# A two-layer hybrid decoder trunk on one core: plain copies of queries and keys, 128-row score products, decay on ScalarE, and other estimates for the order of the mixer

## The chip, the cores and the metric

The kernel runs on one core of one Trainium2 chip. The metric is the device time of one execution in microseconds (us), less is better. The time before is the median of three runs; one more execution was taken with the hardware profiler, and all rows below are of that one.

## The reference

`x` is 512 tokens of 1024 float32 channels. Each of two layers runs a half-step SwiGLU feed-forward block (2816 wide), a token mixer, and a second feed-forward block, each followed by a layer norm of a scaled residual. The mixer has one input projection, three groups of heads, and one output projection:

```
aq, ak, av, bq, bk, bv, cc = jnp.split(x @ w_in[l], IN_SPLIT_IDX, axis=-1)
o_a = diff_attention(rope(aq), rope(ak), av, lam)        # 6 heads, two maps of 32 channels each
o_b = dilated_attention(rope(bq), rope(bk), bv)          # 6 heads of 64 channels
o_c, v_first = rwkv7_mixer(cc, ...)                      # 4 heads of 64 channels
mix = jnp.concatenate([o_a, o_b, o_c], axis=-1) @ w_out[l]
```

`diff_attention` is causal: softmax of the first map minus `lam` times that of the second, times the values. `dilated_attention` comes down to one causal softmax with a bias by distance. `rwkv7_mixer` is a recurrence over tokens, with `S_t = S_{t-1} (diag(w_t) - kk_t^T (a_t kk_t)) + v_t^T k_t`.

## The kernel before

Products keep float32 accuracy by splits: an operand is a high part (rounded to the type `FR`, fp32r) plus a low part, and a product is high x high + high x low + low x high, three products of TensorE (`mm3`). In the mixer the weights come through SP's queue (`wr`), ScalarE rounds the high part (`wh`) and POOL subtracts the low part (`wl`).

The feed-forward blocks are written in their order. The mixer isn't: it is 24 generators (list `RANK`), each of which yields what its next step needs (a tile, a free buffer, an event) and then issues that step. `Board.merge` runs them once, while the program is built. It keeps a clock for each engine and, by the estimates in `Watched.run` and `Board.note`, a time at which each tile is ready and each buffer is free. It takes the first generator in `RANK` whose needs are met by TensorE's planned time, or else the one whose needs are met first. So the estimates alone set the order of the instructions on all five queues, and each engine then works through its queue in that order. As all calls go through `Watched.run`, the profile puts nearly all of the mixer on one line, L511.

The steps that the change and the prediction touch:

- `columns`, `by_token`: the input projection, in products `p<-...` of 256 columns (groups A and B) and the main filling work of the mixer. `out` is the output projection, in products of 512 columns.
- `turner`: for each of 24 tiles `rc` of queries and keys, two transposes on TensorE, the split into `z` (high part on ScalarE, low on VectorE), and a store by SP into DRAM (`qkA`, `qkB`).
- `fetch`: POOL's queue brings the queries `q` and keys `k` of one head back, with high and low parts stacked on partitions, so that one product of 96 rows (A) or a pair of products (B) gives a split score. The tiles are of type `FR` and the DRAM tensor is float32. Four buffers `x` hold two heads. Group A has four copies for each head, group B three, of which the last brings the low keys into 64 rows.
- `attend`: for each head and each 128 queries, a unit of work: scores into `p`, VectorE adds the bias and finds the maximum (`t`, `nm`), ScalarE takes the exponential, TensorE transposes the result (`m<-kept,t`), ScalarE copies it to `aT`, TensorE multiplies by the values (`r<-v,aT`), VectorE scales (`o`) and ScalarE squares (`junk`). A layer has 24 units of group A and 24 of B.
- `scan`: the recurrence in 8 chunks of 64 tokens. Each chunk has three dependent steps: products into `z`, copied to `zs`; products with the inverse (`r<-zs,t16t`), copied with a changed sign into `uv`; products with `bt` into the new state `st`. `sgm` is the state times the decay of the next chunk, and the next state adds it. `rwkv_out` makes the chunk's output.

The second product of a unit of group B, and the decay:

```
pe.matmul(sc[:, :nn], a[:, 0, qs], a[:, 1, :nn], start=True, stop=False)
pe.matmul(sc[:, :nn], a[0:64, 0, qs], b[:, :nn], start=False, stop=True)
...
vec.tensor_scalar(sgm[:, j, :], nst[:, j, :], gam[j][:, ch + 1:ch + 2], None, op0=OP.mult)
```

Of the kernel before, what the change touches and what calls it, by code (L numbers as in the profile page):

```python
# [16 lines left out]
S = 512  # L17
# [352 lines left out]
class Board:  # L370
# [36 lines left out]
    def note(self, name, fn, aps, cost):  # L407
        at = self.free[name]
        tiles = [self.ready.setdefault(a.tensor.name, [0.0, "", 0.0, None]) for a in aps]
        assert all(r[3] != "dropped" for r in tiles)  # L410
        dma = fn == "dma_start"
        for r in tiles[dma and tiles[0][1] == "dma":]:
            if r[1] != name or name != "pe":
                at = max(at, r[0] + 0.134)
        end = at + cost
        self.free[name] = end
        if dma:
            n = 4
            for d in aps[0].shape:
                n *= d  # L420
            end = max(end, self.free["dma"]) + n / 340e3
            self.free["dma"] = end
            end += 2.0
        for r in tiles:
            r[2] = max(r[2], end)
        tiles[0][0] = max(tiles[0][0], end)
        tiles[0][1] = "dma" if dma else name
        if dma:
            self.late = max(self.late, end)
        elif name != "pe":  # L430
            self.last = max(self.last, end)
# [45 lines left out]
class Watched:  # L477
# [5 lines left out]
    def __getattr__(self, fn):  # L483
        call = getattr(self.engine, fn)

        def run(*args, **kw):
            aps = [a for a in list(args) + list(kw.values()) if hasattr(a, "tensor") and hasattr(a, "shape")]
            n = 1
            for a in aps:
                m = 1  # L490
                for d in a.shape[1:]:
                    m *= d
                n = max(n, m)
            if self.name == "pe":
                n = 1
                for d in aps[0].shape[1:]:
                    n *= d
                rate = 2 if fn == "transpose" else 1 if aps[2].dtype == FR and n >= 256 else 4
                cost = rate * n / 2400.0 + (0.009 if rate == 4 else 0.003)
            elif fn == "dma_start":  # L500
                cost = {"pool": 1.04, "act": 0.5, "sp": 0.47}[self.name]
            elif fn == "reciprocal":
                cost = 0.06 + n / 160.0
            else:
                cost = {"vec": 0.07 + n / 960.0, "act": 0.12 + n / 1400.0, "pool": 0.1 + n / 720.0}[self.name]
                if fn == "activation" and "accum_out" in kw:
                    cost += 0.1
                if fn == "tensor_tensor" and self.name == "pool":
                    cost = 0.1 + n / 450.0
            self.board.note(self.name, fn, aps, cost)  # L510
            return call(*args, **kw)  # L511

        return run
# [7 lines left out]
class Mix:  # L521
# [247 lines left out]
    def fetch(self):  # L769

        dma = self.gps.dma_start
        ap = lambda t, off, dims: bass.AP(tensor=t.tensor, offset=t.offset + off, ap=dims)
        for grp in "AB":
            for hp in range(3):
                for e in range(2):
                    yield f"qk{grp}{hp}", "x", "x"
                    if (hp, e) == (0, 0):
                        yield f"qk{grp}{hp}", "x", "x", "bias"
                        self.bias = self.get("bias", "bias")
                        dma(self.bias, self.tr.consts[:, 130:642] if grp == "A" else self.tr.consts[:, 642:1154])  # L780
                    a = self.get("x", "q", (128, 2, S), FR)
                    d = self.qk[grp, hp]
                    hi, lo, k = e * 64 * S, (256 + e * 64) * S, 128 * S
                    if grp == "A":
                        b = self.get("x", "k", (128, 2, S), FR)
                        dma(a[0:64], ap(d, hi, [[256 * S, 2], [2 * S, 32], [1, 2 * S]]))
                        dma(b[0:64], ap(d, hi + k, [[0, 2], [2 * S, 32], [1, 2 * S]]))
                        dma(a[64:96], ap(d, hi, [[2 * S, 32], [1, 2 * S]]))
                        dma(b[64:96], ap(d, lo + k, [[2 * S, 32], [1, 2 * S]]))
                    else:  # L790
                        b = self.get("x", "k2", (64, S), FR)
                        dma(a[:, 0, :], ap(d, hi, [[256 * S, 2], [S, 64], [1, S]]))
                        dma(a[:, 1, :], ap(d, hi + k, [[0, 2], [S, 64], [1, S]]))
                        dma(b, ap(d, lo + k, [[S, 64], [1, S]]))
                    self.qkt[grp, hp, e] = a, b
                    self.mark(f"q{grp}{hp}{e}")


# [307 lines left out]
    def scan(self):  # L1106

        vec, act, pe, sp = self.vec, self.act, self.pe, self.sp
        u, drop, kr, am, bt, yt, gam = self.u, self.drop, self.kr, self.am, self.bt, self.yt, self.gam
        st = None  # L1110
        yield "yt0"
        for ch in range(8):
            hf, cc = divmod(ch, 4)
            if cc == 0:
                yield "u", "u"
                for j in range(2):
                    kr[j, hf] = u("kr", (128, 4, 2, 64))
                    sp.dma_start(kr[j, hf].rearrange("p c e t -> p (c e t)"), self.kd[j, hf])
                yield f"yt{hf}", kr[0, hf], kr[1, hf]
            yield f"uv{ch // 2}"  # L1120
            uv, vt = self.uv[ch // 2]
            uvc = uv[:, ch % 2]
            heads = [(h, h // 2, HALF[h % 2], HALF[1 - h % 2], am[hf, h % 2, cc // 2][:, cc % 2, h // 2]) for h in range(4)]
            yield ".", "r"
            z = self.acc("r", (128, 2, 64))
            for h, j, s, f, a_ in heads:
                pe.matmul(z[f, j, :], a_[s, 0:64], uvc[s, h, :], start=True, stop=st is None)
                if st is not None:
                    pe.matmul(z[f, j, :], kr[j, hf][s, cc, 0, :], st[s, j, :], start=False, stop=True)
            zs = self.t("zs", (128, 2, 64), bufs=2)  # L1130
            act.copy(zs, z)
            drop(z)
            yield ".", "r"
            ups = self.acc("r", (128, 2, 64))
            for h, j, s, f, a_ in heads:
                pe.matmul(ups[f, j, :], yt[hf][f, cc * 2 + j, :], zs[f, j, :], start=True, stop=True)
            act.mul(uvc[HALF[1], 0::2], ups[HALF[1]], -1.0)
            vec.tensor_scalar(uvc[HALF[0], 1::2], ups[HALF[0]], -1.0, None, op0=OP.mult)
            drop(ups)
            nst = None  # L1140
            if ch < 7:
                yield ".", "r", "st"
                ps = self.acc("r", (128, 2, 64))
                for h, j, s, f, a_ in heads:
                    pe.matmul(ps[s, j, :], bt[hf, cc // 2][:, cc % 2, j, s], uvc[:, h, :], start=True, stop=True)
                nst = self.get("st", "st", (128, 2, 64))
                for j in range(2):
                    gj = gam[j][:, ch:ch + 1]
                    if st is None:
                        vec.tensor_scalar(nst[:, j, :], ps[:, j, :], gj, None, op0=OP.mult)  # L1150
                    else:
                        vec.scalar_tensor_tensor(nst[:, j, :], ps[:, j, :], gj, sgm[:, j, :], op0=OP.mult, op1=OP.add)
                drop(ps)
                if ch < 6:
                    sgm = self.t("sgm", (128, 2, 64), bufs=2)
                    for j in range(2):
                        vec.tensor_scalar(sgm[:, j, :], nst[:, j, :], gam[j][:, ch + 1:ch + 2], None, op0=OP.mult)
            if cc == 3:
                drop(yt[hf], bt[hf, 0], bt[hf, 1])
            self.chunks.append((ch, uv, st, heads, kr, vt, am))  # L1160
            self.mark(f"chunk{ch}")
            st = nst
# [62 lines left out]
    def attend(self, grp):  # L1225
# [6 lines left out]
        def scores(x):  # L1232
# [7 lines left out]
            for m in range(M):  # L1240
                sc = self.acc("p1")
                if isA:
                    pe.matmul(sc[:, :nn], a[0:96, m, qs], b[0:96, m, :nn], start=True, stop=True)
                else:
                    pe.matmul(sc[:, :nn], a[:, 0, qs], a[:, 1, :nn], start=True, stop=False)
                    pe.matmul(sc[:, :nn], a[0:64, 0, qs], b[:, :nn], start=False, stop=True)
                t = self.get("t", "t")
                nm = self.t("nm", (128, 1), bufs=8)
                vec.tensor_tensor_reduce(t[:, :n], sc[:, :n], bias[:, S - n:], scale, 3e38, op0=OP.add, op1=OP.min,
# [300 lines left out]
```

## Time and profile before

| | |
|---|---|
| median of three runs | 2336.14 us (2324.28 to 2336.32) |
| the profiled execution | 2317.18 us, span 2315.4 us |
| TensorE (PE) busy | 2210.5 us, 95% of the span, mean granted clock 0.974 |
| VectorE (DVE), ScalarE (ACT), GpSimd (POOL) busy | 1146.9, 803.2, 317.8 us |
| DMA | 258.34 MB, mean 112 GB/s |
| first mixer, second mixer | about 376 to 818 us, 1520 to 1968 us |

The span runs from the first to the last instruction of the profiled execution. A busy TensorE is not TensorE at its peak: a matmul at the lower clock, or one that is started late after the one before it, counts as busy. The list of waits puts idle time of an engine down to what ended it; in the list by lines and in the timeline a name such as `p<-k,q` reads output<-inputs, then the tile of the array (rows x columns), the shape, and the count. A float32 product that isn't `FR` is two rows in the trace, a transpose or an `FR` product one. Without that in mind, a mean over rows is half the time of such a product.

### The profile page before, as it was taken

The numbers are of one execution on the slowest core, as the hardware profiler recorded it, in microseconds if no ns is written. First come the engines' busy times: TensorE is split into PE (matmuls) and PEld (weight loads), VectorE is DVE, ScalarE is ACT, GpSimd is POOL, SyncE is SP. The second block draws the span as 40 slices with busy tenths as digits, with TensorE's granted clock in tenths as the row PEclk, the third lists the DMA queues.
The fourth block names the chain that finished last, engine by engine and source line by source line (L and its number), as shares of the span: only waits on it lengthen the run. The fifth ranks groups of instructions, "written<-read, shape, count | busy, mean of one in ns | idle before, by whom it ended". The sixth has DMA issues, their size and how long they took to land.

```text
span 2315.4 us, 31736 instructions
## 1 busy us (share of the span) xinstructions
PE 2210.5 (95%) x12384; PEld 1861.4 (80%) x12384; DVE 1146.9 (50%) x2483; ACT 803.2 (35%) x1559; POOL 317.8 (14%) x344
## 2 busy tenths in 40 slices
PE   9999999987899999999999999999878999999998
PEld 8888888787776788888888888887877867888886
DVE  3333337766666733333643332556665666333336
ACT  3332223434445322322433222343444443222222
POOL 1000002443222200000010000033432322000000
PEclk9999999998889999999999999999987999999999
DMA  5333344354533333332543333432554433333334
GB/s 171 100 97 103 105 137 155 101 136 84 117 93 107 110 91 91 100 100 91 173 120 103 102 101 109 152 131 86 134 107 96 107 95 119 86 97 91 100 109 155
DMA packets 265702, 258.34 MB, mean 112 GB/s; under 512 B 56314, under 2 KB 213056, under 8 KB 265552
## 3 DMA queue, kind: packets, MB, share of 16 engines
q1 hardware_dynamic: 221488, 228.20, 32.6%
q0 software_dynamic: 43488, 27.06, 5.7%
q8 instruction: 97, 1.59, 0.3%
q10 hardware_dynamic: 576, 1.05, 0.1%
q14 instruction: 53, 0.43, 0.1%
HBM read 233.85 MB, written 22.28 MB: 111 GB/s over the span
## 4 chain that ended last, share of the span: by engine, by line
PE 82%; DVE 8%; DMA 5%; issue 3%; POOL 1%; ACT 1%; SPq 0%; DVEq 0%; POOLq 0%; ACTq 0%
PE p L86 18%; PE p L87 18%; PE p L85 18%; PE p L511 14%; PE r L511 4%; PE m L511 4%; DMA k<-qkA 3%; PE r L86 2%; PE r L87 2%; PE r L85 2%; DMA k<-qkB 1%; DVE x L511 1%; POOL wl L511 1%; DVE xlo L511 1%; DVE gy L511 0%
## 5 line engine op out<-in xcount | busy, mean ns | idle before, releaser
L80 DVE TENSOR_TENSOR lo<-raw,hi 128x1024 fp32r<-128x1024 f32 x300 | 366.1, 1223 | 626.8 <-ACT hi L79 626.6
L86 PE MATMUL p<-xlo,hi 128*128 128x512 f32 (+1 forms) x1392 | 534.7, 384 | 0.7 <-DVE xlo L126 0.7
L85 PE MATMUL p<-xhi,hi 128*128 128x512 f32 (+1 forms) x1392 | 531.4, 382 | 0.5 <-ACT xhi L125 0.5
L87 PE MATMUL p<-xhi,lo 128*128 128x512 f32 (+1 forms) x1392 | 531.6, 382 | 0.0
L79 ACT CAST hi<-raw 128x1024 fp32r<-128x1024 f32 x300 | 315.1, 1052 | 582.7 <-PE p L86 256.6
L85 PEld LDWEIGHTS p<-xhi,hi 128*128 128x128 f32 x1392 | 261.3, 188 | 55.9 <-ACT xhi L125 1.0
L86 PEld LDWEIGHTS p<-xlo,hi 128*128 128x128 f32 x1392 | 261.5, 188 | 52.4 <-DVE xlo L126 1.1
L87 PEld LDWEIGHTS p<-xhi,lo 128*128 128x128 f32 x1392 | 261.5, 188 | 51.2
L511 POOL TENSOR_TENSOR wl<-wr,wh 128x512 fp32r<-128x512 f32 x152 | 204.1, 1363 | 670.8 <-ACT wh L511 639.5
L511 PE MATMUL p<-wh,xhi 128*128 128x256 f32 (+1 forms) x704 | 234.0, 332 | 2.3 <-DVE rb L511 2.0
L511 PE MATMUL p<-wh,xlo 128*128 128x256 f32 (+1 forms) x704 | 219.1, 311 | 0.5 <-DVE xlo L511 0.4
L511 PE MATMUL p<-wl,xhi 128*128 128x256 f32 (+1 forms) x704 | 218.7, 311 | 0.0
L86 PE MATMUL p<-lo,hh 128*128 128x512 f32 x528 | 205.8, 390 | 0.0
L87 PE MATMUL p<-hi,hl 128*128 128x512 f32 x528 | 205.8, 390 | 0.0
L85 PE MATMUL p<-hi,hh 128*128 128x512 f32 x528 | 205.7, 390 | 0.0
L511 PEld LDWEIGHTS p<-wh,xhi 128*128 128x128 f32 x704 | 139.7, 198 | 13.7 <-PE p L511 2.3
L511 PEld LDWEIGHTS p<-wh,xlo 128*128 128x128 f32 x704 | 139.1, 198 | 7.6 <-DVE xlo L511 2.2
L246 DVE TENSOR_TENSOR hr<-p,hr 128x512 f32<-128x512 f32 x88 | 60.8, 691 | 166.9 <-PE p L87 156.7
L511 PEld LDWEIGHTS p<-wl,xhi 128*128 128x128 f32 x704 | 139.5, 198 | 4.3
L247 ACT CAST hh<-hr 128x512 fp32r<-128x512 f32 x88 | 54.3, 618 | 205.8 <-DVE hr L246 195.8
L511 ACT ACTIVATE t<-t,nm 128x128 f32<-128x128 f32 (+3 forms) x144 | 80.1, 557 | 120.7 <-DVE nm L511 119.7
L85 PEld LDWEIGHTS p<-hi,hh 128*128 128x128 f32 x528 | 99.1, 188 | 20.5
(253 smaller groups left out, 3054.6 us busy)
## 6 DMA issues: line engine op xcount, KB each, us to landing
raw<-in_ffn_a_down SPq DMA_DIRECT2D x66, 512.0 KB, 3.3
raw<-in_ffn_b_down SPq DMA_DIRECT2D x66, 512.0 KB, 3.3
raw<-in_ffn_a_gate SPq DMA_DIRECT2D x44, 512.0 KB, 3.8
raw<-in_ffn_a_up SPq DMA_DIRECT2D x44, 512.0 KB, 3.8
raw<-in_ffn_b_gate SPq DMA_DIRECT2D x40, 512.0 KB, 3.8
raw<-in_ffn_b_up SPq DMA_DIRECT2D x40, 512.0 KB, 3.8
wr<-in_w_in SPq DMA_DIRECT2D x56, 256.0 KB, 3.2
wr<-in_w_in SPq DMA_DIRECT2D x24, 512.0 KB, 3.7
```

The lines of the kernel that those rows point to most:

```text
L79: nc.scalar.copy(hi, raw)
L80: (vec or nc.vector).tensor_tensor(lo, raw, hi.bitcast(FT), op=OP.subtract)
L85: mm(out, lh, rh, start=first, stop=False)
L86: mm(out, lh, rl, start=False, stop=False)
L87: mm(out, ll, rh, start=False, stop=last)
L246: nc.vector.tensor_tensor(hr, acc[1, f], hr, op=OP.mult)
L247: nc.scalar.copy(hi, hr)
L511: return call(*args, **kw)
```

## The change

Queries and keys are copied into float32 tiles, which are then read as `FR` without a conversion. In group B the low keys are copied twice, into 128 rows, and the second product of a unit takes 128 rows: the high and low parts of the query times the low part of the key. The decay `sgm` is a scaled copy on ScalarE. And the planner's estimates for TensorE, for transfers, and for POOL's issues are others.

```
-            end = max(end, self.free["dma"]) + n / 340e3
+            end = max(end, self.free["dma"]) + n / 300e3
...
-                rate = 2 if fn == "transpose" else 1 if aps[2].dtype == FR and n >= 256 else 4
-                cost = rate * n / 2400.0 + (0.009 if rate == 4 else 0.003)
+                if fn != "transpose" and aps[2].dtype == FR and n >= 256:
+                    cost = n / 2286.0 + 0.0055
+                else:
+                    m = 1
+                    for d in aps[1].shape[1:]:
+                        m *= d
+                    cost = max(n, m) / 1200.0 + 0.004
...
-                cost = {"pool": 1.04, "act": 0.5, "sp": 0.47}[self.name]
+                cost = {"pool": 0.65, "act": 0.5, "sp": 0.47}[self.name]
...
-                    a = self.get("x", "q", (128, 2, S), FR)
+                    a = self.get("x", "q", (128, 2, S))
...
-                        b = self.get("x", "k", (128, 2, S), FR)
+                        b = self.get("x", "k", (128, 2, S))
...
-                        b = self.get("x", "k2", (64, S), FR)
+                        b = self.get("x", "k2", (128, S))
...
-                        dma(b, ap(d, lo + k, [[S, 64], [1, S]]))
-                    self.qkt[grp, hp, e] = a, b
+                        dma(b, ap(d, lo + k, [[0, 2], [S, 64], [1, S]]))
+                    self.qkt[grp, hp, e] = a.bitcast(FR), b.bitcast(FR)
...
-                        vec.tensor_scalar(sgm[:, j, :], nst[:, j, :], gam[j][:, ch + 1:ch + 2], None, op0=OP.mult)
+                        act.activation(sgm[:, j, :], nst[:, j, :], AF.Copy, scale=gam[j][:, ch + 1:ch + 2])
...
-                    pe.matmul(sc[:, :nn], a[0:64, 0, qs], b[:, :nn], start=False, stop=True)
+                    pe.matmul(sc[:, :nn], a[:, 0, qs], b[:, :nn], start=False, stop=True)
```

How this moves instructions shows at two places. The first is TensorE's queue at the end of the second layer's scan. Before, the last step of its second chunk from the end (`r<-uv,bt`) stood amid the scores of group B (`q`, `k_16199`), between the products with the inverse and the transposes of a unit:

```order
L511 MATMUL r<-zs,t16t 64x64 x4
L511 MATMUL m<-kept,rc 128x128 x2
L511 MATMUL m<-kept,o 128x128 x4
L511 MATMUL p_16367<-q 128x256
L511 MATMUL p_16367<-k_16199,q 128x256
L511 MATMUL r<-uv,bt 64x64 x4
L511 MATMUL m<-kept,t 128x128 x2
```

Now it stands behind the last score, and three products of the output projection are what lies between the steps:

```order
L516 MATMUL m<-kept,o 128x128 x4
L516 MATMUL r<-zs,t16t 64x64 x4
L516 MATMUL p_16224<-wh,xhi 128x512
L516 MATMUL p_16224<-wl,xhi 128x512
L516 MATMUL p_16224<-wh,xlo 128x512
L516 MATMUL r<-uv,bt 64x64 x4
```

So the two last chunks of that scan have moved behind the attention of group B.

The second place is ScalarE's queue in the first layer's scan, where `sgm` now stands between the square of one unit and the split of the next turned tile, with exponentials (`t,l<-t,nm`) around it:

```order
L516 ACTIVATE t,l<-t,nm 128x256 x2
L516 COPY aT<-m 128x512
L516 ACTIVATE junk,ssA<-r 128x64
L516 ACTIVATE sgm<-st,gam 128x64 x2
L516 CAST z<-m 128x256
L516 CAST wh<-wr 128x512 x2
L516 ACTIVATE t,l<-t,nm 128x384 x2
```

Before, a row `TENSOR_SCALAR sgm<-st,gam 128x64 x2` stood in VectorE's queue, right behind the new state.

## Rows read from the trace of the kernel before

**Rows 1.** The page: busy time, share of the span and instructions of each engine.

```profile
PE 2210.5 (95%) x12384; PEld 1861.4 (80%) x12384; DVE 1146.9 (50%) x2483; ACT 803.2 (35%) x1559; POOL 317.8 (14%) x344
```

**Rows 2.** Stages: length, busy PE, PEld, DVE, ACT, POOL; clock, DMA, GB/s.

```profile
376.00:818.00 442.00, 397.20 (x2994) 345.51 (x2993) 290.24 (x878) 186.41 (x527) 144.47 (x149) 0.94 0.41 110
818.00:1520.00 702.00, 701.42 (x3189) 581.14 (x3188) 281.75 (x362) 211.74 (x250) 13.61 (x22) 1.00 0.37 112
1520.00:1968.00 448.00, 402.98 (x3003) 348.30 (x3002) 291.67 (x884) 190.91 (x532) 143.59 (x146) 0.94 0.42 108
```

**Rows 3.** TensorE's waits: us in total, times, longest.

```profile
PE p L511 <- DMA k<-qkA: 39.7, 6, 11.0
...
PE r L511 <- ACT junk L511: 4.9, 4, 2.2
...
PE p L511 <- DMA k<-qkB: 0.5, 2, 0.3
```

**Rows 4.** TensorE's timeline at the two longest waits (start, duration; idle before).

```profile
548.59 0.77 PE L511 MATMUL p<-k,q 96*128 96x256 f32 x2 [11.03 <-DMA k<-qkA]
...
1699.86 0.77 PE L511 MATMUL p<-k,q 96*128 96x256 f32 x2 [10.87 <-DMA k<-qkA]
```

**Rows 5.** Eight short stretches of the mixers, with columns as in rows 2.

```profile
504.00:512.00 8.00, 4.83 (x28) 4.82 (x29) 3.48 (x18) 2.23 (x9) 0.00 (x0) 0.79 0.65 125
548.00:556.00 8.00, 7.41 (x45) 7.37 (x46) 4.77 (x20) 3.21 (x12) 0.00 (x0) 0.59 0.18 51
592.00:604.00 12.00, 12.00 (x77) 11.32 (x75) 8.27 (x32) 5.79 (x20) 2.69 (x2) 0.57 0.06 17
632.00:648.00 16.00, 15.68 (x97) 12.05 (x96) 6.02 (x29) 6.45 (x22) 1.72 (x2) 0.57 0.29 64
1656.00:1664.00 8.00, 6.38 (x29) 6.31 (x30) 4.10 (x22) 2.77 (x11) 0.00 (x0) 0.57 0.66 111
1700.00:1708.00 8.00, 8.00 (x66) 7.87 (x67) 4.68 (x20) 3.52 (x15) 0.00 (x0) 0.69 0.17 45
1740.00:1752.00 12.00, 9.63 (x67) 9.05 (x68) 5.92 (x27) 5.00 (x18) 0.25 (x1) 0.61 0.18 49
1780.00:1800.00 20.00, 19.53 (x113) 15.61 (x114) 7.75 (x33) 8.28 (x28) 2.71 (x2) 0.57 0.31 63
```

**Rows 6.** DMA issues on POOL's queue: count, size, median us to landing.

```profile
x<-x POOLq DMA_DIRECT2D x8, 512.0 KB, 4.1
...
k<-qkA POOLq DMA_DIRECT2D x12, 256.0 KB, 12.8
...
bias<-in_constants POOLq DMA_DIRECT2D x4, 256.0 KB, 3.4
```

**Rows 7.** Chain, 527 to 552 us; then POOL by line (count, busy us, mean ns).

```profile
529.39 18.95 DMA k<-qkA
...
L511 POOL DMA_DIRECT2D k<-qkA x24 | 15.4, 641 | 0.0
```

**Rows 8.** TensorE's timeline in group B, layer 0, 714 to 722 us.

```profile
714.63 1.00 PE L511 MATMUL r<-v,aT 128*128 128x64 f32 x8
...
717.66 0.36 PE L511 MATMUL p<-q 128*128 128x256 f32 x1
717.95 0.38 PE L511 MATMUL p<-k,q 64*128 64x256 f32 x1
718.26 0.55 PE L511 MATMUL m<-kept,t 128*128 128x128 f32 x3
```

**Rows 9.** The same for group A, layer 1, 1706 to 1725 us.

```profile
1714.47 0.40 PE L511 MATMUL p<-k,q 96*128 96x256 f32 x2
1714.71 0.49 PE L511 MATMUL m<-kept,t 128*128 128x128 f32 x3
```

**Rows 10.** VectorE's timeline, 622 to 634 us; then ScalarE by line, first mixer.

```profile
626.48 3.95 DVE L511 TENSOR_SCALAR sgm<-st,gam 128x64 f32<-128x64 f32 x2
...
L511 ACT ACTIVATE uv<-r 64x128 f32<-64x128 f32 x8 | 2.2, 272 | 2.3 <-PE r L511 2.1
```

## The prediction

> **What bounds the kernel now.** The page first: TensorE is busy for 2210.5 us of a span of 2315.4 us [rows 1], so little can be won except where it idles or runs slowly. The table by stage shows where that is [rows 2]. The feed-forward stretch between the mixers (702 us) has TensorE busy for all but 0.6 us at a granted clock of 1.00. The two mixers (442 and 448 us) have it busy 397.20 and 402.98 us at a mean clock of 0.94. So 44.8 + 45.0 = 89.8 us of idle time lie in the mixers, and more is lost there to the clock.
>
> The list of TensorE's waits names the largest piece [rows 3]: 39.7 us in 6 waits for the transfer that brings keys of group A from DRAM, three in each layer. The longest, 11.03 and 10.87 us, stand ahead of the scores of the second pair's first head [rows 4]. After each such wait the clock is granted at its lower level, 1.2 GHz, for a while: six of the eight windows of [rows 5] begin at such a wait. Busy time times (1 - clock) is what they lose: 1.0 + 3.0 + 5.2 us in layer 0 and 2.7 + 2.5 + 3.8 in layer 1, 18.2 together. The other two windows, 632 to 648 and 1780 to 1800, follow the 2.2 us waits for "junk" on ScalarE [rows 3] and lose 6.7 and 8.4 us, 15.1 together.
>
> **The change, part by part.**
>
> *Plain copies.* A converting copy of 256 KB from POOL's queue lands 12.8 us after its issue; on the same queue, copies without conversion land in 3.4 us (256 KB) and 4.1 us (512 KB) [rows 6]. I take 3.4 for each, and 4.1 as the bound for a queue under load. One of them, with POOL's splits of weights right behind its issue, took 18.95 us [rows 7]. Two of the six waits take 11 us, the other four (39.7 - 21.9) / 4 = 4.5 us on average. Those ahead of the first pair go: the copy lands 9.4 us sooner, while the new order puts 24 projection products less between the last turned tile and the scores (84 for 108 in layer 0), 2.9 us at 0.12 us each, the half of two products with as many columns [rows 9]; 6.5 us are left of the gain. The long waits go too: from the release of the first head's tiles to the scores now lie 78 products of 0.12 us in layer 0, 9.4 us without the other work, against four issues of 0.64 us [rows 7] and a landing of 3.4, 6.0 us. I leave 4 us for places where POOL's in-order queue makes the issue late, since its splits of weights stand ahead of the fetches. So -36 us of waits (bounds 0, if the conversion is not what is slow, and -40), and -15 of the 18.2 us at the lower clock (bounds 0 and -18).
>
> What is late next at these places is VectorE's work on the same tiles, and SP's store of the turned tile that the fetch must follow. Each of the 12 fetches of group B carries 128 KB more, since its low keys now fill 128 rows. The units of the head before it hide that, and TensorE waited 0.5 us in all for these keys even when they were converted [rows 3]; I cost it at nothing, and with the cover gone at 12 x 0.7 us (4.1 less 3.4), 8 us.
>
> *128-row products.* A unit of group B has one product of 128 rows and one of 64. With 256 columns, the 64-row product starts 0.29 us after the other, and the next work 0.31 us after that [rows 8], 0.60 us in all, though nothing is waited for. Two products of 96 rows with as many columns take 0.24 us from start to start of the next work [rows 9]. The tile of 64 rows starts only when the one before it is through, and the one after waits again. So 0.36 us per unit, 48 units, -17.3 us if all of it lay on the path. Six units are followed by 64-row work of the scan anyway, and some end in another wait: I take -14 (bounds 0 and -17).
>
> The Trainium skill (TensorEngine Tiling (Array Packing), section Theoretical Speedup) speaks against this edit: a contraction of 64 or less can be packed two to the array, up to twice as fast. By it, widening gives up half of the array for these products, and the sum would hold rival D's term instead. The trace does not agree: here a 64-row product takes 0.29 to 0.31 us where a 96-row one takes 0.12 [rows 8, 9].
>
> *Decay on ScalarE.* The 24 small products "sgm" leave VectorE. In layer 0 a pair of them took 3.95 us, beside POOL's issues and splits [rows 10], and layer 1 has one like it; "o" and then "junk" waited behind it, and TensorE behind those. On ScalarE the nearest row, a scaled copy of 64x128, takes 0.27 us [rows 10], 0.54 a pair, against an idle half of ScalarE; the next step of the scan that needs it is a whole chunk away. Up to -4.4 us of waits and -15.1 us of clock. But other VectorE work of the same kind may meet POOL in its place, and small products of the inversion stand there too. I take half, -10 (bounds +6, a ScalarE queue that holds the exponentials up by 0.27 us in 24 places, and -20).
>
> *The order.* The estimates move nearly every row of the mixers; the work stays the same. The other 45 us of idle time (89.8 - 39.7 - 4.9) come from chains on VectorE that remain. TensorE's new spacing for full-precision products is one half of what rows show: four products by "v" are eight rows and 1.00 us [rows 8], while the planner counts 0.111 us each. That puts more filling work ahead of each dependent step than needed early on, and leaves less at the end. I take +10 us for waits that appear elsewhere; the bounds are -12 (a quarter of the 45 us covered) and +26 (half of the copies' 51 us given back, rival B).
>
> **Sum.** -36 - 15 - 14 - 10 + 10 = -65 us. From the profiled execution, 2317.18 us, that is 2252. The runs shown have a median of 2336.14, 19 us more than the profiled one, and no view says which stage has it. I add 8 us, less than half: **2260 us**.
>
> **Rivals.**
>
> A. *The copies are no quicker.* If POOL's queue and not the conversion makes the 12.8 us, the first two terms go: 2317 - 14 - 10 = 2293, with the 8 us 2301. For it: all of these copies are on one queue that POOL itself feeds. Against it: 3.4 and 4.1 us on that very queue. Chance 0.06.
>
> B. *Half comes back as other waits.* With keys on time, the next late thing is VectorE's part of each unit, and a new wait lowers the clock as the old ones did. Half of 51 us returns: 2260 + 26 = 2286. For it: VectorE is busy 290 us of 442 in a mixer, and 45 us of idle time already end on such chains. Against it: the new order puts projections between these steps. Chance 0.19.
>
> C. *Slower: the scan is left for last.* In layer 1 the last two chunks of the scan now stand behind the last score of group B, with one group of three products between dependent steps, where they stood amid scores and projections before. Each chunk has three steps from TensorE to ScalarE or VectorE and back, with a copy of about 0.27 us [rows 10] in each. It decides if bare steps eat up the 65 us: 16 chunks x 3 steps with 1.4 us of wait each would make 67, about 2327. More than 1.4 us a step is needed to pass the old time; at 2 us a step, 96 us, it is 2260 + 96 = 2356. For it: the halved price of full-precision products. Against it: some 87 products of 512 columns still lie between the end of group B and the last turned tile. Chance 0.04.
>
> D. *A widened product costs a second product's time*, 0.12 us a unit [rows 9]: +6 us over 48 units in place of -14, so 2280. Against it: the gaps in [rows 8]. Chance 0.02. The packing rule above would end here.
>
> E. *More comes back.* All bounds at their good ends, with the clock staying up through the mixers: 2317 - 40 - 18 - 17 - 20 - 12 = 2210, with the 8 us 2218, and half way there 2239. For it: most of the removed waits and the clock behind them are the same few events. Against it: 45 us of waits have other causes. Chance 0.14.
>
> **How the numbers follow.** The forecast, 2245 to 2278, has 0.55. The range takes in B and D, most of E and half of A: 2228 to 2300. About 0.5% is what a measurement of this kernel can tell from no change, 12 us. Faster by more than that: the forecast, A, B, D and E but for a little that A and B lose to a bad end, 0.94. Within it 0.03, slower 0.03.
>
> **What would show it.** Right: the keys of group A land 3 to 5 us after their issue; TensorE's wait for them is under 6 us in all; a mixer takes some 30 us less, at a clock of 0.96 or more; no gap beyond 0.15 us between the two products of a unit of group B; no "sgm" on VectorE. Wrong: landings still near 12 us (A); waits on VectorE up by 20 us or more (B); idle time between "zs" and the products of the scan at the end of layer 1 (C).

## The result and the profile after

The changed kernel is slower: 2345.48 us, median of 14 runs (2339.05 to 2351.12), against 2328.73 us for the kernel before in 14 runs beside it. The ratio is 1.0072, 95% interval [1.0055, 1.0089]. The forecast was 2260.

The profiled execution took 2339.98 us. The page's line of busy time, as in [rows 1]:

```profile
PE 2217.7 (95%) x12384; PEld 1868.3 (80%) x12384; DVE 1138.6 (49%) x2459; ACT 810.1 (35%) x1583; POOL 318.9 (14%) x344
```

As many matmuls as before, busy for 7 us more in spite of the wider products; the clock was lower, as the stages show, with the columns of [rows 2] (the limits lie later, since the mixers end later; the first window holds some 10 us of the feed-forward stretch):

```profile
376.00:830.00 454.00, 407.37 (x3033) 355.16 (x3032) 289.01 (x868) 191.22 (x541) 145.60 (x149) 0.92 0.40 109
830.00:1520.00 690.00, 688.43 (x3131) 570.23 (x3130) 278.88 (x358) 208.11 (x244) 9.77 (x19) 1.00 0.37 114
1520.00:1990.00 470.00, 412.47 (x3020) 356.21 (x3019) 287.06 (x873) 195.91 (x547) 147.67 (x148) 0.91 0.38 105
```

The feed-forward stretch is as it was. The mixers' clock fell from 0.94 to 0.92 and 0.91, and more of the second is idle. TensorE's waits say at what, with the columns of [rows 3]:

```profile
PE p L516 <- DMA k<-qkA: 42.9, 6, 11.3
PE m L516 <- DVE xlo L516: 15.5, 8, 3.9
PE r L516 <- DVE rs_y L516: 10.0, 4, 3.7
PE p L516 <- DMA q<-qkB: 7.4, 4, 3.1
...
PE p L516 <- DMA k<-qkB: 4.0, 4, 1.7
...
PE r L516 <- ACT junk L516: 1.6, 3, 1.3
```

The wait that was to vanish, 39.7 us before [rows 3], is 42.9 us. Group B's copies are now waited for too, 7.4 us for the queries and 4.0 for the keys. Before, the keys cost 0.5 us [rows 3], and the queries stood in the list with 0.3:

```profile
PE p L511 <- DMA q<-qkB: 0.3, 2, 0.2
```

So the copies of both groups cost 13.8 us more, about as much as the idle time that the mixers gained (14 us, below). The waits for VectorE, summed over the whole list, rose by less, from 39.0 to 44.2 us. "junk" shrank, 4.9 to 1.6. The DMA issues on POOL's queue (count, size, median us to landing) show why the first did not go:

```profile
q<-qkB POOLq DMA_DIRECT2D x24, 256.0 KB, 10.0
...
q<-qkA POOLq DMA_DIRECT2D x12, 256.0 KB, 13.0
k<-qkA POOLq DMA_DIRECT2D x12, 256.0 KB, 13.7
k<-qkB POOLq DMA_DIRECT2D x12, 256.0 KB, 10.4
...
k<-qkA POOLq DMA_DIRECT2D x12, 128.0 KB, 13.5
```

Without any conversion the keys still land 13.7 us after their issue (12.8 before, [rows 6]). The smaller copies of group A, which stand behind two of 256 KB in POOL's queue, land as late. The timeline has the same two long waits as [rows 4]:

```profile
518.14 0.77 PE L516 MATMUL p<-k,q 96*128 96x256 f32 x2 [11.31 <-DMA k<-qkA]
...
1669.27 0.77 PE L516 MATMUL p<-k,q 96*128 96x256 f32 x2 [10.97 <-DMA k<-qkA]
```

And in the middle of the first of them, the windows view (columns as in [rows 2]) and the DMA view of the same 4 us:

```profile
513.00:517.00 4.00, 0.00 (x0) 0.00 (x0) 0.00 (x0) 0.00 (x0) 0.00 (x0) 0.50 0.53 135
```

```profile
q0 software_dynamic: 230, 0.44, 42.9%
```

No engine computes, the clock is granted at 1.2 GHz (0.50), and POOL's queue (q0: packets, MB, share of 16 engines) moves 0.44 MB on 42.9% of the DMA engines' time. POOL had issued the copies of both heads by 507.1 us. They are under way and slow, while the 16 DMA engines together are busy for 0.53 of the time.

The account of the profiled executions: idle time of the mixers went from 44.8 + 45.0 to 46.6 + 57.5 us (+14), and what the clock takes (busy time times one less the clock, summed over windows of 4 us) from 19.7 + 22.4 to 27.2 + 32.7 us (+18). Less some 10 us for the wider products (an estimate from the 11 us measured below) that is +22; the two executions differ by 22.8.

### The profile page after: what moved, and what is told of

It reads as the page before. It is cut to its first block, busy times and chain, and to the rows that moved or that the text cites. A ratio compares the mean times of both kernels' runs of the same rounds, so it can differ in the third digit from the quotient of the medians.

```text
span 2338.1 us, 31750 instructions
## 1 busy us (share of the span) xinstructions
PE 2217.7 (95%) x12384; PEld 1868.3 (80%) x12384; DVE 1138.6 (49%) x2459; ACT 810.1 (35%) x1583; POOL 318.9 (14%) x344
## 2 busy tenths in 40 slices
DMA packets 258790, 259.95 MB, mean 111 GB/s; under 512 B 50938, under 2 KB 207680, under 8 KB 258640
## 3 DMA queue, kind: packets, MB, share of 16 engines
q8 instruction: 97, 1.59, 0.3%
## 4 chain that ended last, share of the span: by engine, by line
PE 79%; DVE 10%; DMA 6%; ACT 2%; issue 2%; POOL 1%; SPq 0%; DVEq 0%; POOLq 0%; ACTq 0%
PE p L87 18%; PE p L85 18%; PE p L86 18%; PE p L516 13%; PE r L516 4%; DMA k<-qkA 3%; PE m L516 3%; DMA k<-qkB 2%; PE r L86 2%; PE r L85 2%; PE r L87 2%; DVE x L516 1%; DVE t L516 1%; DVE x L146 1%; DVE x L150 0%
## 5 line engine op out<-in xcount | busy, mean ns | idle before, releaser
L516 PEld LDWEIGHTS p<-wh,xhi 128*128 128x128 f32 x704 | 139.4, 198 | 13.5 <-ACT xhi L516 3.8
L86 PEld LDWEIGHTS p<-lo,hh 128*128 128x128 f32 x528 | 99.1, 188 | 20.5
```

What stands on the lines that cost most here:

```text
L86: mm(out, lh, rl, start=False, stop=False)
```

## The experiments

Each ratio is to the kernel before, run beside it on the same chip, with its 95% interval.

**Conversion alone.** The tiles become float32 and are read as `FR`, queries and both tiles of keys; the order of all queues is that of before.

```
-a = self.get("x", "q", (128, 2, S), FR)
+a = self.get("x", "q", (128, 2, S))
...
-self.qkt[grp, hp, e] = a, b
+self.qkt[grp, hp, e] = a.bitcast(FR), b.bitcast(FR)
```

> The kernel before with float32 tiles for queries and keys (no conversion in the copy) and nothing else; every engine's order is as before. Theory few engines (a copy whose DRAM side begins with a dimension of two is carried by few of the 16 DMA engines, whether it converts or not): copies of 256 KB from qkA still land 12 to 14 us after their issue, TensorE waits 35 to 45 us for k<-qkA, the time is within 0.3% of before. Rival conversion (the prediction's): landings of 3.4 to 5 us, the waits under 8 us, 35 to 55 us less.

Measured: 2325.28, ratio 1.0009 [0.9986, 1.0032]. TensorE's waits and the landing:

```profile
PE p L511 <- DMA k<-qkA: 38.5, 6, 9.2
```

```profile
k<-qkA POOLq DMA_DIRECT2D x12, 256.0 KB, 12.3
```

The conversion is not what makes these copies slow.

**Split copies.** In the kernel before, each copy whose outermost dimension is two is issued as two copies; the planner is told of one, so the order stays.

```
-dma(b[0:64], ap(d, hi + k, [[0, 2], [2 * S, 32], [1, 2 * S]]))
+two(b[0:64], b[0:32], b[32:64], (d, hi + k), 0, [[2 * S, 32], [1, 2 * S]])
```

The queries, and the two copies of group B with an outermost two, go likewise.

> The kernel before, with its converting copies, but each copy whose DRAM side begins with a dimension of two is issued as two copies with 32 or 64 rows outermost; the planner is told of one copy at the old price, so the order of all engines stays but for POOL's added issues. Theory few engines: the last copy of a head lands within 4 to 7 us of its issue though there are more issues, TensorE's waits for k<-qkA fall from 40 us to under 12, the clock stays up behind them, 35 to 55 us less than before (ratio 0.976 to 0.985). Rival POOL's queue or the read back from DRAM is slow in itself: landings stay above 10 us, the waits stay or grow by the added issues (0.65 us each), ratio 0.998 to 1.006.

Measured: 2254.95, ratio 0.9703 [0.9681, 0.9726]: 70 us less with the converting copies of before. No wait for keys is left among the larger ones. The DMA issues:

```profile
q<-qkB POOLq DMA_DIRECT2D x48, 128.0 KB, 3.2
q<-qkA POOLq DMA_DIRECT2D x36, 128.0 KB, 4.6
k<-qkA POOLq DMA_DIRECT2D x36, 128.0 KB, 4.9
k<-qkB POOLq DMA_DIRECT2D x12, 128.0 KB, 3.4
```

By the windows, idle time of the mixers is 23.4 + 22.4 us and the clock takes 8.8 + 10.1: 44 and 23 us less than before. But shape and number of the copies changed together; a later run parts them.

**Estimates alone.** The three estimates of the change in the kernel before.

> The kernel before with the three new estimates (TensorE's spacing, transfers, POOL's issue) and none of the other edits. Theory order (the estimates cost more than the whole change does): 0.8 to 1.6% slower than before, 20 to 35 us, with more waits of TensorE on VectorE's rs_y and on keys. Rival order neutral (the loss comes from the other edits): within 0.4% of before.

Measured: 2373.65, ratio 1.0223 [1.0189, 1.0257]. TensorE's waits:

```profile
PE p L516 <- DMA k<-qkA: 41.7, 5, 12.2
PE m L516 <- DVE xlo L516: 16.1, 7, 4.9
PE p L516 <- DMA q<-qkB: 11.2, 5, 4.2
PE r L516 <- DVE rs_y L516: 9.4, 4, 3.1
```

These are the waits of the changed kernel, without its edits.

**Edits alone.** Plain tiles, 128-row products and decay on ScalarE, with the old estimates; the planner reacts to the edits.

> The change without its estimates: plain copies, 128-row products and the decay on ScalarE, ordered by the estimates of before. Theory order: 0.4 to 1.2% faster than before (10 to 28 us: up to 17 us from the products, up to 19 us from the decay, nothing from the copies). Rival: the edits are what slows, 0.3 to 1% slower than before.

Measured: 2335.23, ratio 1.0039 [1.0013, 1.0064], 9 us more: what the rival expected. Among TensorE's waits:

```profile
PE m L511 <- DVE xlo L511: 17.5, 8, 5.7
PE p L511 <- DMA q<-qkB: 12.3, 4, 4.0
...
PE r L511 <- DVE rs_y L511: 4.3, 2, 2.1
```

The waits for `xlo` and for group B's queries come with this order as well, so they are not the estimates' alone. Of the larger ones only `rs_y` tells the two apart: 4.3 us here as before, 9.4 and 10.0 with the new estimates.

**128-row products alone, low keys in two copies.** Order held.

```
-dma(b, ap(d, lo + k, [[S, 64], [1, S]]))
...
+self.nc.gpsimd.dma_start(b[0:64], ap(d, lo + k, [[S, 64], [1, S]]))
+self.nc.gpsimd.dma_start(b[64:128], ap(d, lo + k, [[S, 64], [1, S]]))
...
-pe.matmul(sc[:, :nn], a[0:64, 0, qs], b[:, :nn], start=False, stop=True)
+pe.matmul(sc[:, :nn], a[:, 0, qs], b[:, :nn], start=False, stop=True)
```

> The kernel before with 128-row products in group B alone; the low keys come as two copies of 64 rows, the planner is told of the old one, so the order of TensorE, VectorE, ScalarE and SP is as before. Theory the pair of tile sizes costs 0.36 us a unit: the 48 units save 10 to 17 us (ratio 0.993 to 0.9955), and in the timeline a pair of 256 columns takes 0.24 us from start to the start of the next work. Rival other waits take it up: within 0.2% of before.

Measured: 2314.72, ratio 0.9952 [0.9926, 0.9978], 11 us less. TensorE's timeline at the unit of [rows 8]:

```profile
716.45 0.36 PE L511 MATMUL p<-q 128*128 128x256 f32 x1
716.65 0.28 PE L511 MATMUL p<-k,q 128*128 128x256 f32 x1
716.76 0.59 PE L511 MATMUL m<-wa,c 128*128 128x256 f32 x2
```

From start to start 0.20 and 0.11 us, where it was 0.29 and 0.31. Group B's copies land no earlier than before, and its queries are waited for in the profiled execution, the slowest of this run:

```profile
PE p L511 <- DMA q<-qkB: 5.7, 3, 3.2
```

```profile
k<-qkB POOLq DMA_DIRECT2D x24, 128.0 KB, 9.6
```

**The same with the low keys in one copy**, as the change has it: `[[0, 2], [S, 64], [1, S]]`.

> As e5_rows_two, but the low keys come as the change brings them, in one copy whose DRAM side begins with a dimension of two. Theory few engines: this copy lands 2 us or more later than the 9.7 us of e1_plain, TensorE waits 6 to 18 us more for q and k of qkB, and the gain of the products is lost: 0 to 0.8% slower than e5_rows_two. Rival: no difference to e5_rows_two beyond 0.2%.

Measured: 2321.59, ratio 0.9989 [0.9962, 1.0015]. The copy of twice the bytes lands in 10.2 us and is waited for:

```profile
PE p L511 <- DMA k<-qkB: 3.7, 3, 1.8
```

```profile
k<-qkB POOLq DMA_DIRECT2D x12, 256.0 KB, 10.2
```

By the medians the one copy gives back 7 of the 11 us, but the two intervals overlap, and the waits do not explain it: with two copies TensorE waited 5.7 us for group B's queries and 1.6 for its keys, here 0.7 and 3.7. What the one copy costs by itself stays open.

**Decay alone.** Order held.

```
-vec.tensor_scalar(sgm[:, j, :], nst[:, j, :], gam[j][:, ch + 1:ch + 2], None, op0=OP.mult)
+act.activation(sgm[:, j, :], nst[:, j, :], AF.Copy, scale=gam[j][:, ch + 1:ch + 2])
```

> The kernel before with the decay on ScalarE alone, the planner told of the old engine, so that only the 24 products change their queue. Theory of the prediction: the two 2.2 us waits for junk go, and half of the 15 us behind them at the lower clock or more: 5 to 19 us less (ratio 0.992 to 0.998). Rival: other VectorE work meets POOL in its place, within 0.15% of before.

Measured: 2326.18, ratio 1.0024 [0.9996, 1.0052]. The waits for "junk" fell to 0.4 us, and those for group B's queries rose to 8.1 us in three. TensorE's timeline at both layers (start, duration; idle before), and the window at the first:

```profile
637.01 0.55 PE L511 MATMUL p<-q 128*128 128x256 f32 x1 [2.75 <-DMA q<-qkB]
...
1790.70 0.55 PE L511 MATMUL p<-q 128*128 128x256 f32 x1 [2.70 <-DMA q<-qkB]
```

```profile
636.00:648.00 12.00, 10.84 (x38) 7.43 (x39) 2.99 (x19) 3.06 (x11) 0.00 (x0) 0.50 0.22 49
```

The wait of 2.2 us moved a few products on, to a copy that was late anyway and had been hidden behind it: the product at 637.01 us starts 8.3 us after VectorE begins the new state (`st`), with the decay on either engine. The clock falls as before.

**The change with split copies.**

> The change, with each copy whose DRAM side begins with a dimension of two issued as two, the planner told of one; the order is that of the change but for POOL's added issues. Theory few engines: landings of 3 to 5 us, TensorE's waits for q and k under 10 us in all (54 us in the change), 50 to 85 us less than the change: ratio to before 0.970 to 0.986. Theory order on top: still 10 us or more above the 2255 us of e2_split though it holds two edits that save, since its estimates leave more waits on VectorE. Rival: with early copies the new estimates are the better ones, below 2245 us.

Measured: 2288.05, ratio 0.9844 [0.9806, 0.9883]. With landings of 3.9 to 4.5 us it is still 33 us above the old order with split copies.

**Everything in the old order.** Split copies, 128-row products with low keys in two copies, decay on ScalarE; the planner is told of the old steps.

> The kernel before, in its own order, with three parts at once: the copies of outer dimension two issued as two, the 128-row score products (their low keys in two copies of 64 rows), and the decay on ScalarE. The planner is told of the old steps at their old prices, so no other instruction moves. Theory (the parts are sound, and what spoiled the change were the shape of its copies and its order): the split gives 2255 as when tried alone, the 128-row products another -10 (they gave -11 alone), and the decay, which gained nothing while the late copies caught the same wait, now -2 to -8: 2235 to 2245, ratio to before 0.963 to 0.968. Rival (the gains overlap: what the products save is idle time that VectorE's chains would fill anyway once the copies are early): 2250 to 2258, ratio 0.970 to 0.973. If the decay on ScalarE holds exponentials up: above 2258.

Measured: 2245.61 (2244.31 to 2250.97), ratio 0.9658 [0.9622, 0.9695], the fastest of all and below both kernels. The page, and the longest of TensorE's groups of waits:

```profile
PE 2184.9 (97%) x12384; PEld 1846.5 (82%) x12384; DVE 1132.7 (50%) x2459; ACT 806.9 (36%) x1583; POOL 334.8 (15%) x404
```

```profile
PE m L511 <- DVE xlo L511: 11.7, 8, 2.4
```

Neither a copy nor "junk" is among the eleven largest groups. The median lies 9 us below the split copies alone; their intervals overlap.

**Which estimate?** Three variants of the change with split copies: the old spacing of TensorE; the old prices of transfers and issues; and full-precision products at the spacing that the trace shows.

```
...
-                    cost = n / 2286.0 + 0.0055
...
+                rate = 2 if fn == "transpose" else 1 if aps[2].dtype == FR and n >= 256 else 4
+                cost = rate * n / 2400.0 + (0.009 if rate == 4 else 0.003)
```

```
-            end = max(end, self.free["dma"]) + n / 300e3
+            end = max(end, self.free["dma"]) + n / 340e3
...
-                cost = {"pool": 0.65, "act": 0.5, "sp": 0.47}[self.name]
+                cost = {"pool": 1.04, "act": 0.5, "sp": 0.47}[self.name]
```

```
+                elif fn != "transpose" and aps[2].dtype != FR:
+                    cost = 0.06 if max(n, m) <= 64 else 0.25
```

> The change with split copies (2288 when tried, ratio 0.984) and the old estimates of TensorE's spacing; the new estimates for transfers and POOL's issues stay. Theory one (the new spacing spoils the order: it counts full-precision products of 128 columns at half of their old price and a quarter to a half of what the trace shows): most of the 33 us by which the split change lies above the old order with split copies comes back, 2245 to 2262, ratio 0.965 to 0.973. Theory two (the prices of moving data spoil it: cheaper issues make the planner put scores before their copies land, which the remaining 3.2 to 3.4 us waits for group A show): it stays at 2280 to 2292, ratio 0.981 to 0.986, with those waits still there.

Measured: 2274.13, ratio 0.9776 [0.9734, 0.9818].

> The other half: the change with split copies and the new spacing, but the old estimates for transfers (340 for 300) and POOL's issues (1.04 for 0.65). Theory one (the spacing): 2280 to 2292 stays, ratio 0.981 to 0.986. Theory two (the prices of moving data): 2245 to 2262, ratio 0.965 to 0.973, and the waits of 3.2 to 3.4 us for group A's copies are gone. If neither half alone gives it back, the order has no single bad estimate, and any new one lands some 30 us above the old order, which would be the best of many.

Measured: 2290.43, ratio 0.9844 [0.9804, 0.9883].

> The change with split copies and its estimates, but full-precision products at the spacing that the trace shows for them (0.25 us with 128 columns or 128 stationary rows, 0.06 for 64x64). Theory one (wrong spacing spoils the order): nearer the trace should be better, 2240 to 2265, ratio 0.963 to 0.974. Theory two (the prices of moving data): 2280 to 2292 stays. Theory three (orders scatter; accuracy of one price means little to a greedy planner): anywhere between, or above 2292.

Measured: 2274.29, ratio 0.9786 [0.9747, 0.9825].

By the medians the spacing makes 14 of the 33 us, though the intervals still touch; the other prices alone give nothing back. A price nearer the trace gives no more than the old one, which counts a product by the values at 0.116 us where rows show 0.25 [rows 8]. So here the accuracy of one price did not carry over to the order.

**The same number of copies in another shape.** The change, in its own order, with the two outer dimensions of each copy exchanged; high and low parts alternate on the partitions of queries and keys alike.

```
-dma(b[0:64], ap(d, hi + k, [[0, 2], [2 * S, 32], [1, 2 * S]]))
+dma(b[0:64], ap(d, hi + k, [[2 * S, 32], [0, 2], [1, 2 * S]]))
```

> The change, with the two outer dimensions of each copy from DRAM exchanged (64 or 32 rows outermost, the two parts inside), so that high and low parts alternate on the partitions, for queries and keys alike; the products sum over partitions and are the same. Number of copies, bytes and the order of all five queues are those of the change. Theory (an outermost dimension of two is what makes the copy slow): landings of 3.5 to 6 us in place of 10.0 to 13.7, no wait over 4 us for queries or keys, 2275 to 2292, ratio to before 0.978 to 0.987, as the split copies gave (0.984). Rival (two copies of half the size are fast because they run beside each other, and one of 256 KB stays slow in any shape): landings of 10 us or more and 2335 to 2350, ratio 1.004 to 1.010.

Measured: 2281.6, ratio 0.9805 [0.9774, 0.9837]. The DMA issues of this run, then the packets of the changed kernel's page, then of this run's:

```profile
q<-qkB POOLq DMA_DIRECT2D x24, 256.0 KB, 4.8
q<-qkA POOLq DMA_DIRECT2D x12, 256.0 KB, 5.0
k<-qkA POOLq DMA_DIRECT2D x12, 256.0 KB, 5.6
k<-qkB POOLq DMA_DIRECT2D x12, 256.0 KB, 4.9
...
k<-qkA POOLq DMA_DIRECT2D x12, 128.0 KB, 6.0
```

```profile
DMA packets 258790, 259.95 MB, mean 111 GB/s; under 512 B 50938, under 2 KB 207680, under 8 KB 258640
```

```profile
DMA packets 231910, 259.78 MB, mean 114 GB/s; under 512 B 24058, under 2 KB 180800, under 8 KB 231760
```

Same tiles, count and order; landings of 13.7 and 10.4 us become 5.6 and 4.9, and 26880 packets are gone, all of them under 512 B (50938 less 24058); only 0.17 MB went with them, some 6 bytes each. The shape was the cause, not the number of copies. POOL's queue hands the delay on: the copies of 128 KB, whose access is as it was (32 rows outermost), stand behind the others and land in 6.0 us in place of 13.5.

**Exchanged dimensions in the old order, and with the old estimates but free to react.**

> The kernel before in its own order, with exchanged dimensions in place of split copies, 128-row score products with their low keys in one copy, and the decay on ScalarE; the planner is told of the old steps. Against the same with split copies (2246, ratio 0.966) it has 60 issues of 0.64 us fewer on POOL. Theory (the shape): as fast as that, 2238 to 2248, ratio 0.962 to 0.967; the 60 issues lay beside other work and give at most 5 us. Rival (number of copies): landings over 10 us and 2305 to 2325, ratio 0.992 to 1.000.

Measured: 2257.3, ratio 0.9707 [0.9678, 0.9736]: a miss by some 10 us, though its interval overlaps that of the split version. In both layers TensorE waits for "junk" again (1.33 and 1.59 us), and the clock falls to 0.50 behind it. VectorE's timeline ahead of the first (start, duration):

```profile
600.30 3.13 DVE L511 SCALAR_TENSOR_TENSOR rs_y<-rs_t,rs_y 128x8 f32<-128x8 f32 x1
```

The median of this operation is 0.16 us. It stands beside POOL's issues and splits, as "sgm" did in [rows 10], and both end where POOL's splits end (POOL's timeline, before and here):

```profile
627.77 2.59 POOL L511 TENSOR_TENSOR wl<-wr,wh 128x512 fp32r<-128x512 f32 x2
```

```profile
600.47 2.94 POOL L511 TENSOR_TENSOR wl<-wr,wh 128x512 fp32r<-128x512 f32 x2
```

That is 630.36 us for POOL and 630.43 for "sgm", 603.41 and 603.43 here; the second layer shows the same. With the split copies it met no such place. Against the profile of that version (everything in the old order) the mixers have 1.5 us more of idle time, and the clock takes 7 us more.

> All edits of the change with the old estimates, and exchanged dimensions: the planner sees the new steps at its old prices and moves some 350 rows of TensorE's queue. With the slow copies this order gave 2335 (ratio 1.004). Theory (the old order was one of many that had been tried, and any shift of it loses waits on VectorE that it had covered): 2258 to 2280, ratio 0.971 to 0.981, well above the pinned order. Rival (only the new estimates spoil the order): 2240 to 2252, ratio 0.963 to 0.968, as the pinned order.

Measured: 2262.93, ratio 0.9732 [0.9711, 0.9754]. Letting the planner react to the edits costs at most a little (2257.3 to 2262.9); the new estimates cost the other 19 us (to 2281.6). The two profiled executions lie 24 us apart; by the windows, 7 are idle time (51.6 to 58.6 us in the mixers) and 15 the clock (31.6 to 46.9).

## Why the forecast was wrong

*Plain copies (-36 and -15).* This is the step that failed: "A converting copy of 256 KB from POOL's queue lands 12.8 us after its issue; on the same queue, copies without conversion land in 3.4 us (256 KB) and 4.1 us (512 KB)". The copies compared there differ in two things, and the sum put the whole difference down to the conversion. It is the other one: in the code of `fetch`, the DRAM side of the copies that land in 12.8 us has an outermost dimension of two, that of the two quick ones has partitions outermost. The plain copies gave 0 (ratio 1.0009), and the same copies with 32 or 64 rows outermost land in 4.8 to 5.6 us. The trace of before could not have told this by itself, since copies with 32 and 64 rows outermost landed late there too:

```profile
k<-qkA POOLq DMA_DIRECT2D x12, 128.0 KB, 12.5
...
k<-qkB POOLq DMA_DIRECT2D x12, 128.0 KB, 9.5
```

They stand behind the misshapen ones in POOL's queue, and with those put right they land in 6.0 (exchanged) and 3.4 us (split). The 18.95 us of [rows 7], which the prediction takes for a copy of 256 KB, belong to one of these: POOL's fourth issue for that head. The Trainium skill (DMA: Bandwidth & Descriptors, section Rules for kernel authors) says that the slowest dimension sets how many DMA engines carry a copy, so that a leading zero-stride broadcast of a few copies confines it to as few. The runs agree as far as they go: moving the dimension of two inwards took the landings from 13.7 to 5.6 us. No row counts the engines of one copy. The Trainium skill (DMA: Bandwidth & Descriptors, section Rules for kernel authors) also advises against splitting a transfer by halves of the partitions, since the halves serialize. For copies of this shape the measurement differs: split, they land in 3.2 to 4.9 us.

The size of the term was too small, if anything: once the copies land early, 44 us of idle time and 23 us of clock go, against 36 and 15.

Rival A had the sign to look for ("landings still near 12 us") and half a mechanism: POOL's queue is not slow in itself, but hands the delay of a copy on to those behind it. At 0.06 it was too small for a term on which 51 of 65 us hung. Its sum also leaves out the +10 for the order; with it, it comes to 2311, not 2301.

*Low keys in 128 rows (0, bound 8).* One copy in place of two takes the ratio from 0.9952 to 0.9989, near the bound of 8 us, but the intervals overlap. The wait for these keys goes from 0.5 [rows 3] to 3.7 us, so the cover was thinner than forecast; that this wait is what the one copy cost is not shown. The forecast counted the copy at 4.1 us, and it landed in 10.2.

*128-row products (-14).* Confirmed: -11 us (5 to 17 by the interval), gaps of 0.20 and 0.11 us. Rival D, the product at full price, is out.

*Decay (-10, bounds +6 and -20).* The 3.95 us beside POOL's work and the wait for "junk" went as said, and the time did not: what is late next, group B's queries, was not on the list of the sum, since this wait had hidden them. The +5 us is not clear of zero. Whether the decay gains anything with early copies was not measured apart.

*The order (+10, bounds -12 and +26).* Mis-sized: alone, the estimates cost 2.2%, some 50 us, outside the bounds. On top of the edits it is less (1.0039 to 1.0072, and 19 us once the copies land early): the terms do not add. Rival B is not what happened: it had the keys on time, and its sign, waits on VectorE up by 20 us, is not there. `rs_y` (4.2 to 10.0 us) and `xlo` (11.3 to 15.5) grew, but the whole list for VectorE by 5 us, against 14 for copies. With early copies its kind of wait shows: 46.2 us for VectorE in the order of the change, 40.4 in the old one. Rival C, the only slower one, isn't what happened: no wait for "zs" over 0.4 us is in the changed kernel's list, though the second mixer is the one that grew more.

With 0 for the copies, some -3 for the products with their low keys in one copy, +5 for the decay alone and the forecast's own +10 for the order, the sum is about +12, near the measured +17. That is partly luck, since the order alone cost 50 and the terms do not add. Of the 82 us between -65 and +17, the copies' term makes 51.

## What to carry to other kernels

Before a slow transfer is put down to its kind, compare it with a fast one that differs in that alone, and read the access of both in the code: here a dimension of two standing outermost cost 5 to 8 us a copy and held up the sound copies behind it in the queue, and exchanging two dimensions took that away. A removed wait is worth what the next late thing leaves of it, so list what lands or ends just behind it. And in a merge that picks greedily by estimated times, an order that runs well is worth holding while steps are edited: every new order tried here, with better prices or worse, had a median above the old one's with the same copies.

## What the runs showed of the hardware that was not expected

- A converting copy by POOL's queue takes as long as a plain one: 12.8 [rows 6] against 12.3 us with the same shape, and 3.2 to 4.9 against 3.9 to 4.5 us when split.
- In the changed kernel a copy of 256 KB with an outermost dimension of two lands in 10.0 to 13.7 us, with 32 or 64 rows outermost in 4.8 to 5.6, and with the former the page counts twice the packets under 512 B (50938 against 24058).
- Copies behind such ones in POOL's queue land as late, whatever their own shape: 13.5 us for 128 KB with 32 rows outermost, and 6.0 once the copies ahead are exchanged.
- A VectorE operation of 0.16 us took 3.13 us beside POOL's issues and splits, and ended within 0.1 us of POOL's last split, as "sgm" did before. Which operation meets such a place changes with the order, so moving one away does not end it.
